# A decoder layer on one core: the first four weight steps by output block instead of by input chunk

## The chip, the cores and the metric

One core of a Trainium2 chip runs the whole program. The metric is the time of one execution on the device, in microseconds (us); before the change its median over three runs is 1454.42.

## The reference

One inference step of one layer of a hybrid decoder, for 256 prompt tokens and 8 sample tokens together (264 columns, `N`). All arithmetic is float32. What matters here is the very beginning, the combined projection of the normalized input:

```python
xn = rmsnorm(x, g_mix)          # x * rsqrt(mean(x*x) + eps) * g_mix
z = xn @ w_in                   # D = 2048 rows in 16 chunks of 128; 41 output blocks of 128 columns
xr, conv_new = causal_conv(z[..., OFF_RGX:OFF_RGG], conv_buf, conv_w, conv_b)
```

Behind it come an RG-LRU group, an mLSTM group, an output projection, cross attention over 256 memory tokens and a SwiGLU part.

## The kernel before

**Arithmetic.** Every float32 operand of a matmul is split into a high and a low half (type `fp32r`), and each product takes three matmuls: high by high, high by low, low by high (`mm3`). High halves are copies made by ScalarE (`act.activation(..., AF.Copy)`), low halves differences made by VectorE. For x the copy carries the norm weight `g_mix` of its chunk as a scale (`split`); the factor rsqrt(mean) is applied later, when a result leaves PSUM, so the sum of squares (`acc_x`) is not needed at once.

**Steps.** The program is a list of weight steps, each of up to 1 MB of weights: `load_piece` brings a step's two halves from HBM on SP's queue (tile `raw`, five buffers of 512 KB), `split_half` turns each half into high and low (tile `w`, four buffers), and TensorE multiplies. Splits run one step ahead (`LS = 1`), loads three steps ahead (`LD = 3`). Behind the start a step is one output block of 128 columns with all 16 chunks, 48 matmuls.

**The first four steps** differ, since x is not there yet. Step q holds chunks 4q to 4q+3 of x for the first four output blocks, again 48 matmuls, into four banks of PSUM (`first`). In HBM the step's weights lie as [partition, block n, chunk c, 128]. `load_first(i, c)` fetches the weights of one chunk for all four blocks, so each partition reads four runs of 512 B. `pe_first` goes by chunk outside and by block inside, so the first chunk of x and its 256 KB of weights already give 12 matmuls. `split_first` converts in the same order: a chunk of x, then that chunk's weights, eight pairs for two steps. Loads of x (`load_x`, tile `xres`) alternate with those of weights on SP's queue; chunk 0 of x and the first 16 columns of `vec` (they hold `g_mix`, tile `vecs`) come on ScalarE's queue, x first. Before all that TensorE runs eight float32 matmuls of ones on ones (`warm`), which use a tile that VectorE fills.

**Squares.** Chunks 0 to 7 of x are squared one at a time on ScalarE and added on VectorE, behind the split that is the latest one when the loop is at step 1 (`sumsq`). Chunks 8 to 15 come as two batches of four behind the split of step 4 (`last_squares`), and `norm_x` then has TensorE sum `acc_x` over the partitions inside step 5, at its chunk 9.

**Order.** SP's queue is in the order of the code. For the other engines a scheduler decides, except where `in_order()` (ScalarE and VectorE) or `manual_schedule` (TensorE, here from step 4 to step 6) keep the code's order.

Of the kernel before, what the change touches and what calls it, by code (L numbers as in the profile page):

```python
# [10 lines left out]
F32 = mybir.dt.float32  # L11
# [83 lines left out]
def layer_kernel(ctx: ExitStack, tc, xT, memT, vec, wrg, w_in, w_out, w_q, w_k, w_v, w_o,  # L95
# [12 lines left out]
    def in_order():  # L108
        return tc.manual_schedule(engines={mybir.EngineType.Activation, mybir.EngineType.DVE})
# [8 lines left out]
    def B(shape, dt=F32):  # L118
        return sb.tile(shape, dt, tag="B", bufs=NB, name=nm("B"))
# [85 lines left out]
            dve.tensor_sub(wl[:, :nch], r[:, :nch], wh[:, :nch].bitcast(F32))  # L205
        splits[i, h] = (wh, wl)

    def load_first(i, c):

        if c % 2 == 0:  # L210
            raws.setdefault(i, []).append(raw_half())
        r = raws[i][c // 2][:, c % 2 * 512: c % 2 * 512 + 512]
        sp.dma_start(r.rearrange("p (n m) -> p n m", m=P),
                     steps[i][0].rearrange("p (n c m) -> p c n m", c=4, m=P)[:, c])

    def split_first(i, h):

        wh, wl = wrows(sb.tile([P, WW], F32R, tag="w", bufs=4, name=nm("w")), i)
        r = raws[i][h].rearrange("p (c m) -> p c m", m=P)
        with tc.high_priority(), in_order():  # L220
            for c in range(2):
                x, k = 4 * i + 2 * h + c, slice(4 * c, 4 * c + 4)
                split(*xn(x), xres[:, x, :], V("g_mix", x))
                st["split"] = act.activation(wh[:, k], r[:, k], AF.Copy)
                dve.tensor_sub(wl[:, k], r[:, k], wh[:, k].bitcast(F32))
        splits[i, h] = (wh, wl)

    def last_squares():

        a, b = (B([P, BW])[:, 0: 4 * N] for _ in range(2))  # L230
        for t, q in ((a, 2), (b, 3)):
            act.activation(t, xres[:, 4 * q: 4 * q + 4, :].rearrange("p c n -> p (c n)"), AF.Square)
        dve.tensor_add(a, a, b)
        dve.tensor_add(a[:, 0: 2 * N], a[:, 0: 2 * N], a[:, 2 * N:])
        dve.tensor_add(a[:, 0: N], a[:, 0: N], a[:, N: 2 * N])
        dve.tensor_add(acc_x, acc_x, a[:, 0: N])

    def wrows(w, i):

# [32 lines left out]
    def mm3(ps, a, b, start, stop):  # L272
        ah, al = a
        bh, bl = b
        ps, bh, bl = by2(ps), turn(bh), turn(bl)
        pe.matmul(ps, ah, bh, start=start, stop=False)
        pe.matmul(ps, ah, bl, start=False, stop=False)
        pe.matmul(ps, al, bh, start=False, stop=stop)
# [58 lines left out]
    def warm(n, w=None):  # L337

        ps = bank()
        for _ in range(n):  # L340
            pe.matmul(ps[:, :P], ones if w is None else w.to_broadcast([P, P]), ones, start=True, stop=True)

    warm(8)
    onesr = const.tile([P, P], F32R, name="onesr")
    mask = const.tile([P, P], F32, name="mask")
    pick = const.tile([P, 2 * H - 1], F32, name="pick")
# [6 lines left out]
    def V(name, j=0, w=1):  # L353
        o = _V[name][0] + j
        return vecs[:, o: o + w]
# [648 lines left out]
    def pe_first(q):  # L1004
        def f(i):
            w = W(i)
            for c in range(4):
                for n in range(4):
                    mm3(first[n][:, :N], w(4 * c + n), rx(4 * q + c), q + c == 0, q + c == 6)
        return f  # L1010

    def evac_first(_):
# [425 lines left out]
    def load_x(e, lo, hi):  # L1438
        e.dma_start(xres[:, lo:hi, :], xT[:, lo:hi, :])

    for c in range(4):
        load_first(0, c)
        if c == 0:
            load_x(sp, 1, 2)
        elif c == 1:
            load_x(sp, 2, 4)
    for i in range(1, 3):
        for c in range(0, 4, 2):
            load_x(sp, 4 * i + c, 4 * i + c + 2)
            load_first(i, c)  # L1450
            load_first(i, c + 1)
        if i == 1:
            sp.dma_start(vecs[:, 16:], vec[:, 16:])
    with tc.high_priority(), in_order():
        load_x(act, 0, 1)
        act.dma_start(vecs[:, 0:16], vec[:, 0:16])
        act.activation(warm_act, ones[:, 0:1], AF.Square)
        split_half(0, 0)
        split_half(0, 1)
# [4 lines left out]
    for i, (src, cols, pef, evf, need) in enumerate(steps):  # L1464
        if i > 1:
            load_piece(i + LD - 1)
        if i == 7:
            st["rg"] = side(rg_gen(), 0)
        if "pend" in need:
            with tc.high_priority(300):  # L1470
                for e, x in pend:
                    e(x)
            pend = []
        for q in need:
            if q in st:
                finish(lambda: st[q].done)
        if not 4 <= i < 7:
            with tc.high_priority(300):
                for e, x in pend:
                    e(x)  # L1480
            pend = []
        if i == len(steps) - 1:
            kept.enter_context(tc.manual_schedule(engines={mybir.EngineType.PE}))
        now = pe.clock
        dve.clock, act.clock = max(dve.clock, now), max(act.clock, now)
        split_half(i + LS, 0)
        if i + LS < len(steps) and steps[i + LS][1] > 1024:
            split_half(i + LS, 1)
        if i == 4:
            kept.enter_context(tc.manual_schedule(engines={mybir.EngineType.PE}))  # L1490
        ps = pef(i)
        if i == 6:
            kept.close()
        if i == 1:
            with tc.issue_after(st["split"].ins):
                for c in range(8):
                    sumsq(acc_x, xres[:, c, :], c == 0)
        if i == 3:
            with tc.issue_after(st["split"].ins), tc.high_priority():
                last_squares()  # L1500
            st["rstd_x"] = Gen(norm_x())
        if evf is not None:
            pend.append((evf, ps))
        if i == 0:
            for c in range(0, 4, 2):
                load_x(sp, 12 + c, 14 + c)
                load_first(3, c)
                load_first(3, c + 1)
        else:
            load_piece(i + LD)  # L1510
        pump(pe.clock + SLACK)
        if i == 24:
            st["ng"] = side(ml_norm(), 6)
        if i == 57:
            PACE["full"] = False
        if i == 44:
            pool_e.dma_start(kept_k, ml["kb"])
            for q in range(2):
                pool_e.dma_start(kept_v[q], ml["vts"][q])
        if i == 40:  # L1520
            st["memg"] = side(mem_gen(), 7)
# [117 lines left out]
```

## Time and profile before

| what | us |
|---|---|
| median of three runs (lowest, highest) | 1454.42 (1454.29, 1455.89) |
| profiled execution: span from first to last instruction | 1452.1 |
| median less this span | 2.3 |
| TensorE busy | 1439.9 |
| VectorE, ScalarE busy | 1046.0, 793.6 |

The page gives the profiled execution's own time only as its span. In its rows PE is TensorE's matmul side, PEld its weight loads, DVE VectorE, ACT ScalarE, POOL GpSimd, SP the sync engine; a q behind a name is the queue of that engine's own issues. A row of the timeline has its start, its duration, the engine, the source line (L60 is a helper that issues all operations), the operation with out<-in by tile name, and how many like it were merged; in brackets stands how long the engine was idle before it and what ended that. Busy times of TensorE are modelled from pipelined matmuls, so a pause shows as a gap between starts rather than as a small share.

### The profile page before, as it was taken

What the parts mean: (1) busy time and instruction counts of PE and PEld (TensorE: products, weight loads), DVE (VectorE), ACT (ScalarE), POOL (GpSimd) and SP (SyncE); (2) the same over time, 40 slices, a digit from 0 to 9 for tenths busy, and PEclk for the clock granted to TensorE, in tenths of its full rate; (3) what the DMA queues carried; (4) which work ended last, traced back from release to release, by engine and by line L of the source; (5) the groups of instructions that cost most, each with busy time, mean ns of one, the idle gap of its engine ahead of it and who ended that gap; (6) DMA issues with size and microseconds to landing.
All of it is one profiled execution on the core that took longest, in us unless ns stands there. A gap on an engine that the chain in (4) does not pass through costs nothing.

```text
span 1452.1 us, 30115 instructions
## 1 busy us (share of the span) xinstructions
PE 1439.9 (99%) x12059; PEld 1415.4 (97%) x12059; DVE 1046.0 (72%) x1999; ACT 793.6 (55%) x1279; POOL 129.4 (9%) x206
## 2 busy tenths in 40 slices
PE   9999999999999999999999999999999999999997
PEld 8999999999999999999999999999999999999997
DVE  7966798898899999977676665555665655556564
ACT  7678686665556666656544444344444434444463
POOL 0001210000124343410000000000000000000000
PEclk9999999999999999999999999999999999999999
DMA  9755897558799977956555565655555655656573
GB/s 289 234 171 187 289 356 259 175 171 280 268 328 360 340 287 288 361 175 203 191 196 195 194 199 192 199 193 197 194 199 193 196 198 193 199 191 198 165 239 126
DMA packets 100765, 329.18 MB, mean 227 GB/s; under 512 B 11056, under 2 KB 19936, under 8 KB 100624
## 3 DMA queue, kind: packets, MB, share of 16 engines
q1 hardware_dynamic: 84336, 271.95, 56.3%
q0 software_dynamic: 15424, 54.22, 10.4%
q8 instruction: 94, 1.54, 0.4%
q10 hardware_dynamic: 864, 1.09, 0.2%
q14 instruction: 47, 0.39, 0.1%
HBM read 314.36 MB, written 12.86 MB: 225 GB/s over the span
## 4 chain that ended last, share of the span: by engine, by line
PE 56%; issue 2%; DVE 2%; DMA 1%; POOL 0%; ACT 0%; DVEq 0%; POOLq 0%; ACTq 0%
PE mm L60 55%; PE ax L60 1%; DVE B L60 1%; DMA B<-kcT 1%; DVE dw L60 0%; DVE w L60 0%; POOL ds L1189 0%; ACT B L60 0%; ACT dw L60 0%; ACT w L60 0%; POOL B L1243 0%; DVE t L60 0%; DVE c L60 0%; POOL o_v L1287 0%; ACT ds L60 0%
## 5 line engine op out<-in xcount | busy, mean ns | idle before, releaser
L60 PE MATMUL mm<-B,w 128*128 128x264 f32 (+1 forms) x10960 | 1282.1, 279 | 0.5 <-DVE w L60 0.5
L60 PEld LDWEIGHTS mm<-B,w 128*128 128x128 f32 x10960 | 1262.1, 189 | 8.3 <-DVE w L60 0.9
L60 DVE TENSOR_TENSOR w<-raw,w 128x1024 fp32r<-128x1024 f32 (+1 forms) x522 | 625.2, 1199 | 308.2 <-ACT w L60 307.4
L60 ACT ACTIVATE w<-raw 128x1024 fp32r<-128x1024 f32 (+1 forms) x522 | 535.1, 1028 | 518.9 <-PE mm L60 352.1
L60 PE MATMUL mm<-w,B 128*128 128x512 f32 x384 | 86.6, 380 | 0.0
L60 PEld LDWEIGHTS mm<-w,B 128*128 128x128 f32 x384 | 70.7, 189 | 9.4
L1528 POOL TENSOR_TENSOR B<-B,rstd 128x264 f32<-128x264 f32 x4 | 2.8, 736 | 802.8 <-ACT rstd L60 802.8
L60 DVE TENSOR_TENSOR t<-mm,rstd 128x264 f32<-128x264 f32 x96 | 41.4, 432 | 28.5 <-PE mm L60 28.3
L60 DVE SCALAR_TENSOR_TENSOR B<-B,dw 128x256 f32<-128x256 f32 x128 | 53.4, 470 | 3.2 <-ACT dw L60 3.0
L60 DVE TENSOR_TENSOR xres<-xres,mm 128x264 f32<-128x264 f32 (+1 forms) x81 | 34.2, 424 | 29.2 <-PE mm L60 29.2
L60 DVE SCALAR_TENSOR_TENSOR dw<-B,qsm,dw 128x256 f32<-128x256 f32 x96 | 49.1, 516 | 1.7 <-ACT dw L60 0.9
L1189 POOL TENSOR_TENSOR ds<-dw,ds 128x256 fp32r<-128x256 f32 x32 | 36.1, 1128 | 106.0 <-ACT ds L60 96.9
L60 PE MATMUL ax<-B,B 128*128 128x256 f32 (+3 forms) x280 | 44.4, 301 | 0.0
L60 PEld LDWEIGHTS ax<-B,B 128*128 128x128 f32 x280 | 39.0, 191 | 2.2
L60 ACT ACTIVATE B<-xres,vecs 128x264 fp32r<-128x264 f32 (+1 forms) x64 | 32.2, 502 | 3.2 <-DVE xres L60 1.7
L60 ACT ACTIVATE t<-xres 128x264 f32<-128x264 f32 (+1 forms) x53 | 21.0, 408 | 15.9 <-DVE xres L60 15.9
L60 ACT ACTIVATE dw<-B,qsm 128x256 f32<-128x256 f32 x32 | 16.2, 507 | 22.8 <-issue 10.0
L1178 POOL DMA_DIRECT2D B<-kcT x32 | 17.3, 541 | 116.4 <-DVE B L60 103.3
L60 ACT ACTIVATE dw<-B,B 128x128 f32<-128x128 f32 x64 | 21.0, 391 | 11.7 <-DMA B<-scr 9.1
L60 DVE SCALAR_TENSOR_TENSOR B<-xres,vecs,B 128x264 fp32r<-128x264 f32 x48 | 23.4, 489 | 4.0 <-ACT B L60 3.9
L60 ACT ACTIVATE dw<-ax,dw 128x256 f32<-128x256 f32 x32 | 15.0, 471 | 18.7 <-DVE dw L60 16.6
L60 ACT ACTIVATE B<-t 128x264 fp32r<-128x264 f32 (+1 forms) x60 | 24.1, 409 | 2.1 <-DVE t L60 2.1
(173 smaller groups left out, 693.2 us busy)
## 6 DMA issues: line engine op xcount, KB each, us to landing
raw<-w_gu SPq DMA_DIRECT2D x176, 512.0 KB, 4.2
raw<-w_d SPq DMA_DIRECT2D x80, 512.0 KB, 4.3
raw<-w_in SPq DMA_DIRECT2D x74, 512.0 KB, 5.2
raw<-w_out SPq DMA_DIRECT2D x32, 512.0 KB, 4.1
B<-kcT POOLq DMA_DIRECT2D x32, 512.0 KB, 8.8
raw<-w_q SPq DMA_DIRECT2D x32, 512.0 KB, 5.8
B<-vcT POOLq DMA_DIRECT2D x32, 512.0 KB, 9.6
raw<-w_k SPq DMA_DIRECT2D x32, 512.0 KB, 5.2
```

What stands on the lines that cost most here:

```text
L60: return f(*a, **k)
L1178: pool_e.dma_start(kc, kcT[h, b])
L1189: pool_e.tensor_sub(ws[:, 1], acc, ws[:, 0].bitcast(F32))
L1528: e.tensor_mul(st["y"](c), st["y"](c), r)
```

## The change

It does six things. (1) The four chunks of a step's weights are loaded by output block: block n of the step is one piece of 2 KB per partition, `load_first(i, n, k)` loads k blocks at once, and from the third block of step 0 on a load takes two blocks, 4 KB per partition. (2) x is loaded in fours (two chunks at the start), and three of the first four chunks' places change: chunks 0 and 1 come on ScalarE's queue behind the norm weights, chunks 2 and 3 second on SP's. (3) `pe_first` goes by block outside and by chunk inside; for the first block of step 0 it does four high by high, four high by low and four low by high. (4) `split_first` converts all four chunks of x first, then the weights, in pieces of two blocks (in step 0 of one block); the high half of the very first piece is copied by VectorE. (5) All squares come in four batches of four chunks, two behind the splits of step 4 (the fifth block) and two behind those of step 5. (6) The warm-up has seven matmuls on a constant that is there at program start. TensorE's order is now kept from step 0 on.

```diff
-    def load_first(i, c):
-
-        if c % 2 == 0:
+    def load_first(i, n, k=1):
+
+        if n % 2 == 0:
             raws.setdefault(i, []).append(raw_half())
-        r = raws[i][c // 2][:, c % 2 * 512: c % 2 * 512 + 512]
-        sp.dma_start(r.rearrange("p (n m) -> p n m", m=P),
-                     steps[i][0].rearrange("p (n c m) -> p c n m", c=4, m=P)[:, c])
+        o = n % 2 * 512
+        sp.dma_start(raws[i][n // 2][:, o: o + k * 512], steps[i][0][:, n * 512: (n + k) * 512])
...
         with tc.high_priority(), in_order():
-            for c in range(2):
-                x, k = 4 * i + 2 * h + c, slice(4 * c, 4 * c + 4)
-                split(*xn(x), xres[:, x, :], V("g_mix", x))
-                st["split"] = act.activation(wh[:, k], r[:, k], AF.Copy)
+            parts = (slice(0, 4), slice(4, 8)) if i == 0 else (slice(0, 8),)
+            if i + h == 0:
+                dve.tensor_copy(wh[:, 0:4], r[:, 0:4])
+            if h == 0:
+                for x in range(4 * i, 4 * i + 4):
+                    split(*xn(x), xres[:, x, :], V("g_mix", x))
+            for k in parts:
+                if i + h + k.start > 0:
+                    st["split"] = act.activation(wh[:, k], r[:, k], AF.Copy)
                 dve.tensor_sub(wl[:, k], r[:, k], wh[:, k].bitcast(F32))
...
+    def squares(q):
+
+        t = B([P, BW])[:, 0: 4 * N]
+        act.activation(t, xres[:, 4 * q: 4 * q + 4, :].rearrange("p c n -> p (c n)"), AF.Square)
+        dve.tensor_add(t[:, 0: 2 * N], t[:, 0: 2 * N], t[:, 2 * N:])
+        if q == 0:
+            dve.tensor_add(acc_x, t[:, 0: N], t[:, N: 2 * N])
+            return
+        dve.tensor_add(t[:, 0: N], t[:, 0: N], t[:, N: 2 * N])
+        dve.tensor_add(acc_x, acc_x, t[:, 0: N])
...
-    warm(8)
+    warm(7, nc.const_aps.tensor(1.0, [P, P], F32))
...
-            for c in range(4):
-                for n in range(4):
-                    mm3(first[n][:, :N], w(4 * c + n), rx(4 * q + c), q + c == 0, q + c == 6)
+            for n in range(4):
+                ps = first[n][:, :N]
+                if q + n == 0:
+                    for k, l in ((0, 0), (0, 1), (1, 0)):
+                        for c in range(4):
+                            pe.matmul(by2(ps), w(c)[k], turn(rx(c)[l]), start=k + l + c == 0, stop=False)
+                    continue
+                for c in range(4):
+                    mm3(ps, w(4 * n + c), rx(4 * q + c), q + c == 0, q + c == 6)
...
     with tc.high_priority(), in_order():
+        act.dma_start(vecs[:, 0:16], vec[:, 0:16])
         load_x(act, 0, 1)
-        act.dma_start(vecs[:, 0:16], vec[:, 0:16])
+        load_x(act, 1, 2)
...
-        if i == 1:
-            with tc.issue_after(st["split"].ins):
-                for c in range(8):
-                    sumsq(acc_x, xres[:, c, :], c == 0)
-        if i == 3:
+        if i in (3, 4):
             with tc.issue_after(st["split"].ins), tc.high_priority():
-                last_squares()
-            st["rstd_x"] = Gen(norm_x())
+                for q in range(2):
+                    squares(2 * i - 6 + q)
+            if i == 4:
+                st["rstd_x"] = Gen(norm_x())
```

What this does to the order can be seen at three places. The first is SP's queue at program start, before (`raw` are weights, `xres` is x, `vecs` the other vectors; a piece in the form 4x128 is read in runs of 512 B):

```order
L213 DMA raw_117<-w_in 128x4x128
L1439 DMA xres<-xT 128x264
L213 DMA raw_117<-w_in 128x4x128
L1439 DMA xres<-xT 128x528
L213 DMA raw_122<-w_in 128x4x128 x2
L1439 DMA xres<-xT 128x528
L213 DMA raw_126<-w_in 128x4x128 x2
L1439 DMA xres<-xT 128x528
L213 DMA raw_130<-w_in 128x4x128 x2
```

And the same queue after:

```order
L213 DMA raw_116<-w_in 128x512
L1450 DMA xres<-xT 128x528
L213 DMA raw_116<-w_in 128x512
L213 DMA raw_120<-w_in 128x1024
L1450 DMA xres<-xT 128x1056
L213 DMA raw_123<-w_in 128x1024
L213 DMA raw_125<-w_in 128x1024
```

Seven loads now bring what thirteen brought, and x of step 1 stands ahead of all its weights. The second place is ScalarE from its first split on, before (`B` are halves of x where `xres` is read, `w` the high weights):

```order
L60 ACTIVATE B_150<-xres,vecs 128x264
L60 ACTIVATE w_147<-raw_117 128x4x128
L60 ACTIVATE B_150<-xres,vecs 128x264
L60 ACTIVATE w_147<-raw_117 128x4x128
L60 ACTIVATE B_150<-xres,vecs 128x264
L60 ACTIVATE w_161<-raw_122 128x4x128
L60 ACTIVATE B_150<-xres,vecs 128x264
L60 ACTIVATE w_161<-raw_122 128x4x128
```

After, from the same place, with step 1 behind it:

```order
L60 ACTIVATE B_143<-xres,vecs 128x264 x4
L60 ACTIVATE w_139<-raw_116 128x4x128
L60 ACTIVATE w_157<-raw_120 128x4x128 x2
L60 ACTIVATE B_169<-xres,vecs 128x264 x4
L60 ACTIVATE w_166<-raw_123 128x8x128
L60 ACTIVATE w_182<-raw_125 128x8x128
```

The four chunks of x stand together ahead of the weights, and one copy has gone to VectorE. The third place is ScalarE around the squares: before, the first of them stood between the weights of step 2 and the x of step 3 (`acc_x` and `t` are single squares):

```order
L60 ACTIVATE w_270<-raw_139 128x4x128
L60 ACTIVATE acc_x<-xres 128x264
L60 ACTIVATE t_331<-xres 128x264
L60 ACTIVATE t_334<-xres 128x264
L60 ACTIVATE t_337<-xres 128x264
L60 ACTIVATE t_340<-xres 128x264
L60 ACTIVATE t_343<-xres 128x264
L60 ACTIVATE t_346<-xres 128x264
L60 ACTIVATE B_359<-xres,vecs 128x264
```

After, the squares stand behind the weights of steps 4 (`w_391`, `w_394`) and 5 (`w_458`, `w_461`):

```order
L60 ACTIVATE w_391<-raw_313 128x8x128
L60 ACTIVATE w_394<-raw_315 128x8x128
L60 ACTIVATE B_445<-xres 128x1056
L60 ACTIVATE B_449<-xres 128x1056
L60 ACTIVATE w_458<-raw_387 128x8x128
L60 ACTIVATE w_461<-raw_389 128x8x128
L60 ACTIVATE B_513<-xres 128x1056
L60 ACTIVATE B_518<-xres 128x1056
```

No square is left ahead of the x of step 3. Behind these places, from the gates of the ninth block on, every engine's list of operations is the same in both kernels.

More of the change, by code (lines that the diff above doesn't have):

```diff
@@ L220, in split_first @@
         with tc.high_priority(), in_order():
-            for c in range(2):
-                x, k = 4 * i + 2 * h + c, slice(4 * c, 4 * c + 4)
-                split(*xn(x), xres[:, x, :], V("g_mix", x))
-                st["split"] = act.activation(wh[:, k], r[:, k], AF.Copy)
+            parts = (slice(0, 4), slice(4, 8)) if i == 0 else (slice(0, 8),)
[7 more added lines that the diff above has]
+                    st["split"] = act.activation(wh[:, k], r[:, k], AF.Copy)
                 dve.tensor_sub(wl[:, k], r[:, k], wh[:, k].bitcast(F32))
         splits[i, h] = (wh, wl)
[L228 to L236, printed above, removed]
+    def squares(q):
[7 more added lines that the diff above has]
+        dve.tensor_add(acc_x, acc_x, t[:, 0: N])
     def wrows(w, i):
@@ L340, in warm @@
         for _ in range(n):
-            pe.matmul(ps[:, :P], ones if w is None else w.to_broadcast([P, P]), ones, start=True, stop=True)
-    warm(8)
+            pe.matmul(ps[:, :P], w, w, start=True, stop=True)
+    warm(7, nc.const_aps.tensor(1.0, [P, P], F32))
     onesr = const.tile([P, P], F32R, name="onesr")
@@ L1439, in load_x @@
         e.dma_start(xres[:, lo:hi, :], xT[:, lo:hi, :])
[L1441 to L1446, printed above, removed]
+    load_first(0, 0)
+    load_x(sp, 2, 4)
+    load_first(0, 1)
+    load_first(0, 2, 2)
     for i in range(1, 3):
[L1448 to L1451, printed above, removed]
+        load_x(sp, 4 * i, 4 * i + 4)
+        load_first(i, 0, 2)
+        load_first(i, 2, 2)
         if i == 1:
@@ L1488, in layer_kernel @@
             split_half(i + LS, 1)
-        if i == 4:
+        if i == 0:
             kept.enter_context(tc.manual_schedule(engines={mybir.EngineType.PE}))
@@ L1504, in layer_kernel @@
         if i == 0:
[L1505 to L1508, printed above, removed]
+            load_x(sp, 12, 16)
+            load_first(3, 0, 2)
+            load_first(3, 2, 2)
         else:
```

## Prediction

> **What bounds the kernel now.** I read the page first, then the chain of waits, then the list of waits cut to the first 60 us, and last the timeline of those microseconds. The page, and of the chain two pieces ahead of 650 and its two longest:
>
> ```profile
> span 1452.1 us, 30115 instructions
> PE 1439.9 (99%) x12059; PEld 1415.4 (97%) x12059; DVE 1046.0 (72%) x1999; ACT 793.6 (55%) x1279; POOL 129.4 (9%) x206
> ...
> 567.91 1.46 POOL ds L1189
> ...
> 615.05 1.30 DVE B L60 x7
> ...
> 650.03 80.33 PE mm L60 x714
> 730.81 707.06 PE mm L60 x6285
> ```
>
> TensorE is busy for 99% of the span, and its order of work is nearly fixed. One matmul with 264 columns costs 80.33 / 714 = 0.1125 us; 707.06 / 6285 gives the same. The change adds no such matmul and takes none away. So the time can move only by what TensorE waits, and the order of every engine behind the squares of x is the same in both kernels. What the start gains or loses is then carried as a shift to the end. The timeline of the start, in a few places (start, duration, engine, idle time before it and its releaser):
>
> ```profile
> 0.90 0.17 DVE L60 MEMSET ones<- 128x128 f32 x1 [0.90 <-PEq L1611]
> ...
> 1.12 3.78 PE L60 MATMUL mm<-ones 128*128 128x128 f32 x16 [1.12 <-DVE ones L60]
> ...
> 1.22 0.45 ACTq L1456 DMA_DIRECT2D vecs<-vec  x1
> ...
> 1.53 0.60 SPq L1439 DMA_DIRECT2D xres<-xT  x1
> ...
> 1.70 1.28 ACT L60 ACT_TABLE_LOAD   x1 [1.70 <-PEq L1611]
> ...
> 4.02 0.52 ACT L60 ACTIVATE B<-xres,vecs 128x264 fp32r<-128x264 f32 x1 [0.82 <-DMA vecs<-vec]
> 4.44 0.61 ACT L60 ACTIVATE w<-raw 128x512 fp32r<-128x512 f32 x1
> ...
> 5.11 1.19 PE L60 MATMUL ax<-B,w 128*128 128x264 f32 x6 [0.21 <-ACT w L60]
> ...
> 6.93 0.52 ACT L60 ACTIVATE B<-xres,vecs 128x264 fp32r<-128x264 f32 x1
> ...
> 11.44 0.94 PE L60 MATMUL ax<-B,w 128*128 128x264 f32 x6
> ...
> 20.98 1.97 ACT L60 ACTIVATE t<-xres 128x264 f32<-128x264 f32 x6
> ...
> 22.86 0.50 ACT L60 ACTIVATE B<-xres,vecs 128x264 fp32r<-128x264 f32 x1
> 23.27 0.61 ACT L60 ACTIVATE w<-raw 128x512 fp32r<-128x512 f32 x1
> ...
> 23.93 0.60 PE L60 MATMUL ax<-B,w 128*128 128x264 f32 x3 [1.10 <-ACT w L60]
> ```
>
> Real work starts at 5.11, and the first matmul of step 3 at 23.93. In between lie steps 0 to 2, 144 matmuls, 16.20 us of work. TensorE has thus lost 23.93 - 16.20 = 7.73 us: 5.11 ahead of the first and 2.62 in gaps, the last of them 1.10 us behind six squares of x on ScalarE. From 23.93 to 40 it pauses no more. The waits and the traffic of the first 40 us (in 1 us slices) say who is late:
>
> ```profile
> ACT w L60 <- DMA raw<-w_in: 4.4, 8, 1.8
> DVE w L60 <- ACT w L60: 3.7, 9, 0.7
> PEld ax L60 <- ACT w L60: 2.3, 4, 1.3
> ...
> GB/s 0 20 242 299 174 335 297 301 348 321 343 319 309 351 312 309 334 314 330 325 311 335 313 360 394 410 377 262 340 94 295 238 197 295 283 324 283 209 266 221
> ```
>
> TensorE waits for ScalarE's copies and these for the loads. From slice 6 on the traffic stands near 325 GB/s, and it steps up to 394, 410 and 377 in slices 24 to 26, when the pieces in 512 B runs end and those in 4 KB runs begin.
>
> **The change part by part.** What counts is when step 3 starts; I follow the one chain that sets it. Prices (count, busy and mean ns), and the time from issue to landing of the first loads of x:
>
> ```profile
> L60 ACT ACTIVATE w<-raw 128x1024 fp32r<-128x1024 f32 x13 | 13.3, 1049 | 4.8 <-PE mm L60 2.9 <-DMA raw<-w_in 1.8
> L60 DVE TENSOR_TENSOR w<-raw,w 128x1024 fp32r<-128x1024 f32 x11 | 13.3, 1221 | 0.6 <-ACT w L60 0.6
> L60 DVE TENSOR_TENSOR w<-raw,w 128x512 fp32r<-128x512 f32 x18 | 12.4, 689 | 3.4 <-ACT w L60 3.1
> L60 DVE SCALAR_TENSOR_TENSOR B<-xres,vecs,B 128x264 fp32r<-128x264 f32 x16 | 7.8, 489 | 4.0 <-ACT B L60 3.9
> ...
> xres<-xT SPq DMA_DIRECT2D x1, 264.0 KB, 4.1
> xres<-xT ACTq DMA_DIRECT2D x1, 132.0 KB, 2.2
> xres<-xT SPq DMA_DIRECT2D x1, 132.0 KB, 2.9
> vecs<-vec ACTq DMA_DIRECT2D x1, 8.0 KB, 2.7
> ```
>
> *First matmul.* The norm weights go first, so by their 2.7 us they land at 3.5 instead of 1.22 + 2.7 = 3.9. ScalarE has one more load to issue ahead of its table load, 0.4, which then ends near 3.4 and hides under that landing. The first chunk of x is split from 3.6 to 4.1, and no ScalarE copy of weights follows that TensorE must wait for. VectorE's copy of 512 elements is not in this trace: at most the 0.69 of a two-input operation of that size, at least nothing, since it runs while ScalarE works. I take 0.5, and a start at 4.3, 0.8 earlier. The warm-up of seven needs 7/8 of 3.78 = 3.3 us, no longer waits for the tile of ones, so it starts near 0.9, and is over at 4.2.
>
> *First output block.* It needs all four chunks of x, four splits at VectorE and then its low weights. The third and fourth chunk land at 5.3 by the sum of the next part (0.81 MB; the row's 4.1 us from SP's second issue at 1.5 would give 5.6). Splits start 0.42 apart on ScalarE, so the fourth is done at 6.3; VectorE's 0.49 and 0.69 follow, to 7.5, and the four matmuls with the low weights end at 8.0. Blocks two to four follow at 12 x 0.1125 = 1.35 each: 12.05. Step 1 can start 0.6 later than its 11.44 of before: what the earlier start gains is lost again here.
>
> *Step 1 sets the path.* It needs four chunks of x and half its weights. With the x, 4 raw pieces of 256 KB, 8 chunks of 132 KB and 8 KB have come (of 1024 bytes): 2.14 MB; with the first half of the weights 2.66 MB. By 4.0 us the slices have moved 0.56 MB, and at 390 GB/s the rest takes 4.05 and 5.4 us: 8.05 and 9.4. Landing is later than that: the 132 KB on SP landed at 1.53 + 2.9 = 4.43, some 0.5 after its 0.54 MB, and the 264 KB behind it by 6.93, 0.9 after its 1.07 MB (6.0). I take 0.65: 8.7 and 10.05. x is split from 8.75 on and ScalarE is free at 10.43; the copy of 1.05 ends at 11.48, VectorE's low half of 1.22 at 12.73 (its own four splits end before), and TensorE goes on at 12.79. It has reached this point at 12.05 + 0.22, so it stalls 0.5. From there 46 matmuls of step 1 and 48 of step 2 end at 12.79 + 10.57 = 23.36.
>
> On the rate this rests on, the row comes first: 325 GB/s in short runs, 394 in long ones. [...]
>
> *Steps 2 and 3.* By the same sum step 2's x (3.95 MB, other vectors among it) lands at 13.35 and its weights (4.48 MB) at 14.7; they are split by 17.5 and wanted at 17.96. Step 3's land by 18.9, are split by 21.5 and wanted at 23.36. The squares no longer stand there, so the 1.10 gap goes. What is late next is only the stall of step 1.
>
> *Queues.* SP issues 14 loads instead of 25 up to those of step 3; they are larger, so the queue reaches the later weights sooner. Later loads wait for the raw tiles to come free, as now. Cost nothing, hidden under the traffic.
>
> *Squares.* Eight single ones and their adds leave the ramp; four batches come instead, two behind the splits of the fifth block and two behind those of the sixth.
>
> ```profile
> 28.87 2.04 ACT L60 ACTIVATE B<-xres 128x1056 f32<-128x1056 f32 x2
> ...
> 35.48 0.43 DVE L60 TENSOR_TENSOR acc_x<-acc_x,B 128x264 f32<-128x264 f32 x1
> ...
> 38.05 0.72 PE L60 MATMUL ax<-ones,acc_x 128*128 128x1 f32 x6
> ```
>
> Now the sum is ready at 35.9 and TensorE asks at 38.05: 2.1 us to spare. After: the sixth block's second half needs the buffer that step 3 frees at 28.8; copy to 29.8, squares (1.02 each, start to start) to 31.9, adds and interleaved low halves to about 34.5; asked for at 38.05 - 0.57 = 37.5. The cover is 3 us, so I cost it at nothing.
>
> **Sum.** 23.93 - 23.36 = 0.57 gained. The profiled execution has 1452.1 of span, and the median of 1454.42 lies 2.3 above it; I keep that: 1454.42 - 0.57 = 1453.8 us. What a measurement here can tell from no change is about 0.2%, 2.9 us.
>
> **The rivals.** (a) *Longer runs bring no faster traffic*, and TensorE now waits for twice as much data at the head of each step. By the row of slices 2.66 MB are there at 10.95 and land at 11.6; copy and low half take it to 13.95. Step 2's weights (4.48 MB, 16.6) come out at 19.6, and 46 matmuls on step 3 starts at 24.8: 0.9 slower, 1455.3. It decides once the rate stays under about 350. For it: half of step 0's pieces have 2 KB runs, which no row prices. Against: slices 24 to 26.
>
> (b) *TensorE's clock halves in the thin first block.* The trace has one such place (a timeline row, then half-microsecond stretches of TensorE; last columns: granted clock, DMA share, GB/s):
>
> ```profile
> 161.78 0.83 PE L60 MATMUL ax<-ones,B 128*128 128x1 f32 x6 [1.56 <-DVE B L60]
> ...
> 162.50:163.00 0.50, 0.50 (x5) 0.66 0.93 107
> 163.00:163.50 0.50, 0.50 (x4) 0.50 0.66 131
> ...
> 166.00:166.50 0.50, 0.50 (x6) 0.93 0.75 180
> ```
>
> A pause of 1.56 us and then tiny matmuls brought 0.50 from about 162.66 to 166.07, as the shares 0.66 and 0.93 tell, so for 3.4 us; the pause of 1.10 at 22.8 left the rate of matmuls as it was. The first block does 1.35 us of work in the 3.7 from 4.3 to 8.0, in pauses of half a microsecond. Half clock for 3.4 us takes 1.7 us, of which the stall of 0.5 is there anyway: 1.2 - 0.57 = 0.6 slower, 1455.0. [...]
>
> (c) *Loads come earlier than I reckon*, step 1 does not stall and step 0 ends at 11.4 as now: step 3 at 11.4 + 10.8 = 22.2, 1.7 gained, 1452.7.
>
> (d) *The stages up to 650 swallow the shift*: ahead of that the chain runs over POOL and DVE as well, as the two pieces show. Their work is released by TensorE's, so I doubt it: 1454.4.
>
> (e) *The sum of squares comes late*: it decides once the sixth block's weights are over 3 us late, and a pause of 2 us with (b)'s half clock costs 3.7: 1454.42 - 0.57 + 3.7 = 1457.6.
>
> **How the numbers follow.** Forecast 0.45, (a) 0.17, (b) 0.12, (c) 0.15, (d) 0.07, (e) 0.04. From (c) less half a microsecond, to (a) with a little spread of the runs (1454.29 to 1455.89), the range is 1452.2 to 1455.9. Faster than 1451.5 only something beyond (c): 0.06; slower than 1457.3 is (e), or (a) with (b): 0.05; within 0.2%: 0.89.
>
> **What would show it.** Right: first real matmul near 4.3, traffic near 390 GB/s from slice 6 on, a short wait of TensorE for `w` near 12.5, step 3 from 23.4, none behind it to 38. Wrong: slices at 325 (a); a granted clock of 0.50 before 15 us (b); step 3 before 22.5 (c); TensorE waiting ahead of the sums of `acc_x` (e).

## The result and the profile after

The changed kernel is slower: 1458.17 us median against 1454.66 us for the kernel before, ratio 1.0025 with a 95% interval of 1.0015 to 1.0036. Measured a second time, it came out at 1456.80 against 1455.03, ratio 1.0012 [1.0003, 1.0021]. The loss is 1.8 to 3.5 us, more than rival (a)'s 0.9 and about as much as rival (e)'s 3.2, but from another cause than either. The profiled execution took 1462.21 us, with a span of 1460.5; it was the longest of its six.

First the page and the piece of the chain that starts the long last run of matmuls (start, duration), to be held against 1452.1 and 650.03 of before:

```profile
span 1460.5 us, 30069 instructions
PE 1443.9 (99%) x12057; PEld 1418.8 (97%) x12057; DVE 1044.9 (72%) x1994; ACT 792.1 (54%) x1266; POOL 129.6 (9%) x206
...
658.26 80.33 PE mm L60 x714
```

From that piece to the end it takes 802.2 us, before 802.1. So in these two traces 8.2 us are lost ahead of it. The timeline of the start says how the first of them went:

```profile
0.84 3.33 PE L60 MATMUL mm<-const-float32-1.0 128*128 128x128 f32 x14 [0.84 <-PEq L1617]
...
4.30 0.43 DVE L60 CAST w<-raw 128x512 fp32r<-128x512 f32 x1 [3.23 <-DMA raw<-w_in]
...
5.56 0.52 ACT L60 ACTIVATE B<-xres,vecs 128x264 fp32r<-128x264 f32 x1 [1.85 <-DMA xres<-xT]
...
6.12 0.59 PE L60 MATMUL ax<-B,w 128*128 128x264 f32 x1 [1.95 <-ACT B L60]
...
6.58 1.33 ACT L60 ACTIVATE B<-xres,vecs 128x264 fp32r<-128x264 f32 x3 [0.51 <-DMA xres<-xT]
...
7.15 7.43 PE L60 MATMUL ax<-B,w 128*128 128x264 f32 x35 [0.44 <-ACT B L60]
...
8.35 2.49 DVE L60 TENSOR_TENSOR w<-raw,w 128x512 fp32r<-128x512 f32 x4
...
12.38 1.22 DVE L60 TENSOR_TENSOR w<-raw,w 128x1024 fp32r<-128x1024 f32 x1
...
15.77 4.21 PE L60 MATMUL ax<-B,w 128*128 128x264 f32 x36
...
26.57 4.21 PE L60 MATMUL ax<-B,w 128*128 128x264 f32 x36
...
40.41 0.72 PE L60 MATMUL ax<-ones,acc_x 128*128 128x1 f32 x6
```

The warm-up ends at 4.17, and TensorE then waits 1.95 us for the first chunk of x. Behind 7.15 three matmuls follow each other by 0.38 to 0.41 us, the pace of ScalarE's copies of x. From 8.34 on TensorE waits for nothing that the profile shows, and yet its matmuls start 0.22 us apart up to 13.22: the 35 from 7.15 on take 7.43 us where 36 take 4.21 later. VectorE has the low halves of all of step 0's weights at 8.35 + 2.49 = 10.84; the first half of step 1's is there at 13.60, and TensorE comes to step 1 only at 15.77. Step 3 starts at 26.57 (before: 23.93), the sums of `acc_x` come at 40.41 (before: 38.05): 2.36 us late. The first loads (KB each, us from issue to landing) and the traffic in 1 us slices:

```profile
xres<-xT SPq DMA_DIRECT2D x1, 264.0 KB, 4.0
raw<-w_in SPq DMA_DIRECT2D x1, 256.0 KB, 3.5
xres<-xT ACTq DMA_DIRECT2D x1, 132.0 KB, 4.2
vecs<-vec ACTq DMA_DIRECT2D x1, 8.0 KB, 3.7
...
GB/s 0 31 137 309 344 336 425 417 406 418 407 425 394 410 401 410 422 422 414 410 406 406 385 397 188 258 213 147 315 98 340 164 53 303 193 82 324 135 16 193
```

From slice 6 to slice 23 the traffic is 385 to 425 GB/s, as forecast. But what was issued first landed later than in the kernel before: the norm weights took 3.7 us instead of 2.7, the first chunk of x 4.2 instead of 2.2.

The other 5.9 us (8.2 less 2.36) lie nearly all between 165 and 195. The three pauses of TensorE there, and its pace behind the last (columns: TensorE's issue and busy time with the count of matmuls, granted clock, DMA share, GB/s):

```profile
164.19 0.83 PE L60 MATMUL ax<-ones,B 128*128 128x1 f32 x6 [1.56 <-DVE B L60]
171.23 1.57 PE L60 MATMUL ax<-B,B 128*128 128x256 f32 x8 [1.82 <-ACT B L60]
186.63 2.18 PE L60 MATMUL ax<-B,B 128*128 128x256 f32 x8 [1.91 <-ACT B L60]
...
185.00:190.00 5.00, 3.37 (x15) 0.74 1.01 405
190.00:195.00 5.00, 5.00 (x27) 0.57 1.03 397
```

Before had the first of these only, and half clock for 3.4 us behind it; here it is half from 187 to about 194. Whether the change makes the other two is a question for the experiments.

### The profile page after: what moved, and what is told of

Same layout as the page of the kernel before. It is cut to its first block, busy times and chain, and to the rows that moved or that the text cites. A ratio compares the mean times of both kernels' runs of the same rounds, so it can differ in the third digit from the quotient of the medians.

```text
span 1460.5 us, 30069 instructions
## 1 busy us (share of the span) xinstructions
PE 1443.9 (99%) x12057; PEld 1418.8 (97%) x12057; DVE 1044.9 (72%) x1994; ACT 792.1 (54%) x1266; POOL 129.6 (9%) x206
## 4 chain that ended last, share of the span: by engine, by line
PE 56%; DVE 1%; issue 1%; POOL 0%; DMA 0%; ACT 0%; DVEq 0%; POOLq 0%; ACTq 0%
PE mm L60 55%; PE ax L60 1%; DVE B L60 1%; DVE dw L60 0%; DMA o_k<-t 0%; DVE w L60 0%; POOL ds L1200 0%; POOL B L1254 0%; ACT B L60 0%; DVE c L60 0%; POOL o_v L1298 0%; DVE t L60 0%; ACT ds L60 0%; DVEq L1622 0%; ACT c L60 0%
```

## The experiments

Three theories for the start, and one for the rest. **C, the clock:** TensorE works at half its pace (0.22 us from start to start instead of 0.11) through the thin first block and beyond. **Q, the queue:** long rows on SP's queue hold back ScalarE's queue, so x comes late (x0 is its first chunk). **V:** it is the norm weights, in short rows, that hold back what stands behind them on ScalarE's queue. **D:** the stage from 150 to 195 us decides, and by itself. Each kernel is listed with its first real matmul, the number of gaps of 0.20 to 0.27 us between the starts of successive matmuls from 5 to 17 us (of real work; the normal gap is 0.11, and a single one of 0.22 also followed waits at full clock, as the three of the first trace of before did), the start of the sums of `acc_x`, and its median and ratio to the kernel before, timed alongside (whose own median was between 1454.65 and 1455.22 each time):

| kernel | first | slow gaps | sums | us | ratio [95%] |
|---|---|---|---|---|---|
| before (first trace, again) | 5.11, 5.22 | 3, 6 | 38.05, 39.35 | 1454.66 | 1 |
| after | 6.12 | 22 | 40.41 | 1458.17 | 1.0025 [1.0015, 1.0036] |
| after, again | 6.08 | 13 | 39.73 | 1456.80 | 1.0012 [1.0003, 1.0021] |
| after, warm-up 12 | 6.02 | 10 | 39.66 | 1456.18 | 1.0006 [0.9994, 1.0019] |
| after, warm-up 20 | 7.96 | 1 | 38.46 | 1454.92 | 0.9999 [0.9990, 1.0008] |
| after, x on SP | 4.98 | 21 | 39.32 | 1457.07 | 1.0017 [1.0008, 1.0026] |
| after, x on SP, warm-up 16 | 6.59 | 5 | 39.37 | 1456.55 | 1.0009 [1.0000, 1.0018] |
| after, 512 B runs | 5.38 | 20 | 39.96 | 1456.29 | 1.0007 [0.9998, 1.0016] |
| before, vecs first | 5.45 | 2 | 38.84 | 1454.58 | 0.9999 [0.9990, 1.0008] |
| before, 2 KB runs | 6.08 | 1 | 36.23 | 1454.07 | 0.9999 [0.9990, 1.0007] |
| the same, x0 on SP | 4.95 | 5 | 36.43 | 1453.61 | 0.9992 [0.9983, 1.0000] |
| the same, squares late | 4.75 | 8 | 37.74 | 1454.76 | 0.9999 [0.9991, 1.0008] |
| before, squares late | 5.19 | 5 | 40.28 | 1457.42 | 1.0017 [1.0008, 1.0025] |

### The clock: a longer warm-up

```diff
-    warm(7, nc.const_aps.tensor(1.0, [P, P], F32))
+    warm(12, nc.const_aps.tensor(1.0, [P, P], F32))
```

> The changed kernel with twelve warm-up matmuls instead of seven; nothing else. Theory C (clock): the pause of 1.95 us ahead of the first real matmul keeps TensorE at half clock until about 13.3, and that is most of the 2.4 us lost by the sums of squares. Then TensorE is busy until about 6.2, reaches full clock by 8 at the latest, step 1 starts near 13.6 instead of 15.77, the sums near 38.2 instead of 40.4, and the ratio to the kernel before falls from 1.0025 to about 1.001. Rival L (landing): the late x alone sets the pace and the clock costs nothing; step 1 starts within 0.3 us of 15.77 and the ratio stays at 1.0025.

The sums came at 39.66 instead of the 38.2 expected, only 0.75 earlier than in the changed kernel. Twelve matmuls end at 5.43; two pauses follow, of 0.58 and 1.36 us, with a single matmul between them, and from 8.95 to 11.19 the gaps are 0.22 again. TensorE's pace (stretch; TensorE's issue and busy time with the count of matmuls, granted clock, DMA share, GB/s):

```profile
4.00:5.00 1.00, 1.00 (x9) 1.00 1.03 336
...
6.00:8.00 2.00, 0.62 (x2) 0.94 1.04 400
8.00:10.00 2.00, 2.00 (x8) 0.50 1.02 375
10.00:12.00 2.00, 2.00 (x15) 0.70 1.02 396
```

The nine matmuls from 4 to 5 us are at full pace already: this warm-up reached it, and behind the two pauses it was gone again. The shares 0.94 and 0.70 put the half clock from about 7.8 to 11.2, so 3.4 us. What this run does not tell is what a warm-up without a pause behind it would give. One of 20 lasts until x is there:

```diff
-    warm(7, nc.const_aps.tensor(1.0, [P, P], F32))
+    warm(20, nc.const_aps.tensor(1.0, [P, P], F32))
```

> The changed kernel with twenty warm-up matmuls instead of seven. In the changed kernel's trace 23 matmuls stand 0.22 us apart from 8.3 to 13.3 us, and 0.11 apart from then on, though every input was ready by 10.9. Theory C, the clock: with TensorE busy up to 7.1 us these matmuls run 0.11 apart, the first output block ends when its last low weights are ready, near 9.5, and step 1 starts near 13.3 instead of 15.77; sums of acc_x near 38.0 instead of 40.4, and 1454.2 to 1455.8 us. Theory Q alone, late first loads without a lasting loss of clock: step 1 stays where the warm-up of twelve left it, 15.0, or moves later with the longer warm-up; 1456 to 1457. Theory D, the stage from 150 to 200 us decides the time: the time does not follow the start.

Its timeline, and TensorE's pace in stretches of 2 us:

```profile
5.74 0.52 ACT L60 ACTIVATE B<-xres,vecs 128x264 fp32r<-128x264 f32 x1 [2.03 <-DMA xres<-xT]
...
6.71 1.33 ACT L60 ACTIVATE B<-xres,vecs 128x264 fp32r<-128x264 f32 x3 [0.45 <-DMA xres<-xT]
...
7.96 4.67 PE L60 MATMUL ax<-B,w 128*128 128x264 f32 x36
...
13.82 0.39 PE L60 MATMUL ax<-B,w 128*128 128x264 f32 x2
```

```profile
8.00:10.00 2.00, 1.89 (x17) 1.00 1.03 385
10.00:12.00 2.00, 2.00 (x20) 1.00 1.00 386
12.00:14.00 2.00, 2.00 (x20) 1.00 1.03 413
```

The same stretches of the changed kernel:

```profile
8.00:10.00 2.00, 2.00 (x10) 1.00 1.01 412
10.00:12.00 2.00, 2.00 (x11) 1.00 1.04 416
12.00:14.00 2.00, 2.00 (x14) 1.00 1.03 402
```

x came no earlier (its copies start at 5.74 and 6.71, against 5.56 and 6.58), and real work began 1.84 us later, at 7.96. Yet step 1 started at 13.82 instead of 15.77, the sums at 38.46 instead of 40.41, and the time is that of the kernel before. This is theory C: 36 matmuls took 4.67 us once TensorE had not paused ahead of them. Against the second trace of the changed kernel, below, the sums gain 1.27 instead of 1.95.

That it is the granted clock shows in the second trace of the changed kernel:

> The changed kernel once more, unaltered, for a second trace of it. What comes from the change must come again: x0 and x1 landing 4 us and more after their issue, over 15 matmuls 0.22 us apart in the first output block, sums of acc_x at 39.5 to 41, without a wait of TensorE for acc_x. What the first trace lost beyond its start (two pauses of 1.8 and 1.9 us behind the scratch round trips between 165 and 190 us, and half clock behind the second) need not: by the theory that this part varies from execution to execution, the stretch from the sums to the last piece of the ramp of mixing steps, 617.9 us in the first trace, lies between 612 and 615 this time. If the change causes it, 616 or more again.

```profile
8.00:10.00 2.00, 1.98 (x9) 0.57 1.04 389
10.00:12.00 2.00, 2.00 (x12) 0.58 1.01 402
12.00:14.00 2.00, 2.00 (x20) 1.00 1.01 406
```

Here the column falls to 0.57 and 0.58 over 8 to 12 us (13 slow gaps, 8.64 to 11.52, where over 15 were expected). The two shares put the half clock from about 8.3 to 11.7, 3.4 us again. In the first trace the column stands at 1.00 throughout the start, though the pace is the same. Nor does it show the slow pace of the warm-up: in the first traces of before and after it stands at 1.00 over the first 5 us, where 16 matmuls took 3.78 us and 14 took 3.33. Why was not shown; at these starts the pace is read from the starts of the matmuls.

Of theory D, the same trace has this:

```profile
163.31 0.83 PE L60 MATMUL ax<-ones,B 128*128 128x1 f32 x6 [1.56 <-DVE B L60]
183.71 1.57 PE L60 MATMUL ax<-B,B 128*128 128x256 f32 x8 [0.30 <-ACT B L60]
```

The pauses of 1.82 and 1.91 have not come again. From the sums to the 714 matmuls it took 651.80 - 39.73 = 612.1, against 617.9 in the first trace; so the 5.9 us do not come with the change each time. The kernel before, traced again, agrees:

> The kernel before once more, unaltered, for a second trace of it: x0 lands 2.2 us after its issue and the norm weights 2.7 (within 0.4), first matmul 5.0 to 5.4, sums of acc_x 37.8 to 38.5. By the theory that the stage from 150 to 190 us varies by itself, its pauses differ from those of the first trace, where there was one of 1.56 us. If the first trace is typical, the stretch from the sums to the last piece of the mixing steps is 612.0 again, within 0.5.

It paused 1.34 and 0.67 us in this stage and needed 649.77 - 39.35 = 610.4 (first trace: 612.0; 612.0 within 0.5 was expected). Its start varies too: step 2 waited 1.00 us for a copy whose load was late, the pause ahead of step 3, behind the squares, came again with 1.07, and its sums came at 39.35, later than the 37.8 to 38.5 expected. The first trace, with a single gap of 1.10, was an early one. So the starts of single traces of one kernel differ by 0.7 (after) to 1.3 us (before), and smaller differences between variants prove nothing.

Nor do the pauses need the change: the kernel before with the norm weights first, the next run, has all three, of 1.55, 1.96 and 1.39 us, and took 614.6 us for the stretch. The second of them:

```profile
169.63 1.58 PE L60 MATMUL ax<-B,B 128*128 128x256 f32 x8 [1.96 <-ACT B L60]
```

### The queue: who holds back x

> The kernel before with one part of the change alone: the norm weights ahead of the first chunk of x on ScalarE's queue. Theory V (the norm weights' rows of 64 B hold up what stands behind them): x lands more than 1 us later than its 3.0, the norm weights at 0.8 + 3.7, first real matmul near 6 instead of 5.11, and the time is 1 us or more longer. Theory Q: SP's rows are 512 B here, so x loses only its 0.4 us of issue, the norm weights land by 3.5, first real matmul at 5.1 or a little earlier, time unchanged within 0.5 us.

```profile
xres<-xT ACTq DMA_DIRECT2D x1, 132.0 KB, 3.1
```

The norm weights ahead of x0, in the kernel before, landed 1.7 us after their issue, x0 3.1; first matmul 5.45 instead of 5.11, the time unchanged. x0 landed at 4.28 instead of 3.03, so 1.25 later: 0.4 of issue, as Q had it, and 0.9 of a longer wait, as V had it. V's other signs (late norm weights, first matmul near 6, a longer time) did not come. The second place in the queue is thus worth 0.9 of the 2.0 us that are to be explained, and V alone does not explain them. Next, the kernel before with nothing changed but the runs in HBM:

```diff
-        sp.dma_start(r.rearrange("p (n m) -> p n m", m=P),
-                     steps[i][0].rearrange("p (n c m) -> p c n m", c=4, m=P)[:, c])
+        sp.dma_start(r, steps[i][0][:, c * 512: c * 512 + 512])
...
+    w_in[0:4] = w_in[0:4].reshape(4, P, 4, 4, P).transpose(0, 1, 3, 2, 4).reshape(4, P, 2048).copy()
```

> The kernel before, with the weights of the first four steps laid out in HBM by chunk, so that each load by chunk reads one run of 2 KB per partition instead of four of 512 B; order, queues and sizes as before. Theory R (longer runs are what the change gains, and the order by block is what it loses): traffic near 400 GB/s instead of 325 from slice 6 on, the waits for loads go, first real matmul between 5.1 and 5.6 (Q: x on ScalarE's queue lands later than 3.0), step 3 starts near 22.5 instead of 23.93, ratio 0.999. Rival (the rate does not matter because ScalarE and VectorE pace the start): step 3 within 0.3 of 23.93, ratio 1.000.

```profile
xres<-xT ACTq DMA_DIRECT2D x1, 132.0 KB, 3.4
...
vecs<-vec ACTq DMA_DIRECT2D x1, 8.0 KB, 3.7
```

x0 now took 3.4 us instead of 2.2 and the norm weights 3.7 instead of 2.7, though both queues issue the same loads in the same order. That is theory Q. SP also issued its loads closer together, the third at 1.72 instead of 2.17; whether the rows or the earlier loads hold back ScalarE's queue is not separated. Theory R held for the start, though not for the first matmul (6.08): step 3 started at 22.39, and TensorE waited for nothing behind 6.08. The time was that of the rival, 0.9999. The changed kernel has long runs and a first matmul at 6.12 too, and its sums come 3.5 to 4.2 us later: what it loses, it loses by the rest of the change. No run here has the order by block alone, so the order, the places of x and the shorter warm-up are not told apart, except as far as the warm-up of 20 does it. The reverse, the changed kernel back in runs of 512 B:

```diff
-        o = n % 2 * 512
-        sp.dma_start(raws[i][n // 2][:, o: o + k * 512], steps[i][0][:, n * 512: (n + k) * 512])
+        for m in range(n, n + k):
+            o = m % 2 * 512
+            sp.dma_start(raws[i][n // 2][:, o: o + 512].rearrange("p (c m) -> p c m", m=P),
+                         steps[i][0].rearrange("p (c n m) -> p n c m", n=4, m=P)[:, m])
...
+    w_in[0:4] = w_in[0:4].reshape(4, P, 4, 4, P).transpose(0, 1, 3, 2, 4).reshape(4, P, 2048).copy()
```

> The changed kernel with its pieces of weights in 512 B runs again (one load for each output block, so six more issues on SP's queue; order of matmuls, of the first loads and of the squares as changed). Theory Q, long runs on SP's queue hold back ScalarE's: norm weights and x0 land 0.7 to 1.2 us sooner, by 3.8 and 4.4 instead of 4.5 and 5.5, the first matmul at 5.0; the traffic then stays near 325 GB/s and the weights of the later steps come later, sums of acc_x at 40 to 42 and a wait for acc_x possible: 1457 to 1460 us. If run length does not matter to ScalarE's queue: x0 at 5.5 again, first matmul at 6.1.

```profile
xres<-xT ACTq DMA_DIRECT2D x1, 132.0 KB, 3.4
vecs<-vec ACTq DMA_DIRECT2D x1, 8.0 KB, 1.7
```

There were seven more issues on SP's queue, not six. The queue did as Q says (1.7 instead of 3.7, 3.4 instead of 4.2, first matmul 5.38). The rest of the expectation was wrong: the time came out at 1456.29, no worse than with long runs. TensorE waited for no load after 7.01, and 20 matmuls ran at half pace as before; that it could not have used faster traffic fits this, but is argued. In the first 12 us the profile's packets on SP's queue average 0.65 KB in the kernel before and 1.76 KB in 2 KB runs (2.86 MB in 4415, 3.27 MB in 1861); by what mechanism ScalarE's queue is held back was not shown.

x0 and x1 ahead of everything on SP's queue, in the changed kernel:

```diff
+    load_x(sp, 0, 2)
     load_first(0, 0)
...
-        load_x(act, 0, 1)
-        load_x(act, 1, 2)
```

> The changed kernel with chunks 0 and 1 of x as the first load on SP's queue, ahead of the weights, and only the norm weights on ScalarE's. [...] Rival B (it is the bytes in flight, whatever the queue): the first weights and the norm weights come later in exchange, first real matmul not before 5.7, ratio 1.002.

x landed 2.9 us after its issue and the first matmul came at 4.98, 1.14 earlier than in the changed kernel and ahead of rival B's 5.7. But step 1 gained no more than that (14.68 instead of 15.77, sums 39.32 instead of 40.41): 20 gaps stayed slow, from 7.46 to 11.89, and chunks 2 and 3, now third on SP's queue, landed at 6.08 instead of 5.29, so that the wait only moved behind the second matmul:

```profile
6.11 0.92 ACT L60 ACTIVATE B<-xres,vecs 128x264 fp32r<-128x264 f32 x2 [1.25 <-DMA xres<-xT]
```

An earlier x alone is worth 0.4 to 1.1 us of the start, by the two traces of the changed kernel, and the time does not tell it from nothing (1.0017, between 1.0025 and 1.0012). With a longer warm-up as well:

> The changed kernel with the first two chunks of x ahead of everything on SP's queue and sixteen warm-up matmuls. With seven of them that order of loads put the first real matmul at 4.98, but 20 matmuls ran 0.22 apart up to 11.9, and step 1 began at 14.68. Theory C: the warm-up ends at 6.2, no matmul from 7 on stands 0.22 apart, step 1 starts at 12.5 and the sums at 37.1, 1 us ahead of the kernel before: 1453.3 to 1454.5 us. If only the loads matter: step 1 at 14.7 or later, 1456 to 1457.5. Theory D: the sums come at 37.1 and the time is still that of the kernel before or more, 1454.5 to 1456.

No run of slow gaps was left, only five single ones beside waits, and step 0 was through by 13.05; but now step 1 waited twice, up to 14.85 (0.77 us for VectorE's low half of `w`). Sums at 39.37: a miss for C's numbers (37.1), not for its pace. That the x ahead of them on SP's queue made its weights late is argued.

The same move in the kernel before with 2 KB runs, x0 alone:

```diff
+    load_x(sp, 0, 1)
     for c in range(4):
         load_first(0, c)
...
-        load_x(act, 0, 1)
         act.dma_start(vecs[:, 0:16], vec[:, 0:16])
```

> The kernel before with its pieces of weights in 2 KB runs (its order of matmuls kept) and the first chunk of x ahead of them on SP's queue, the norm weights alone on ScalarE's. With 2 KB runs alone the first chunk of x landed 3.4 us after its issue and the first matmul came at 6.08, the sums at 36.2. Theory Q: the chunk of x lands by 3.7 and the norm weights by 4.2, first matmul at 5.1 to 5.3, and since the order by chunk needs one chunk at a time the rate stays full: sums at 35.4 if the later loads keep up, 36.2 if they do not. If the place of x in the queues does not matter: first matmul near 6.1. Theory D puts the time at 1453.3 to 1454.4 whichever it is; if the start counts in full, 1451.8 to 1452.6.

First matmul at 4.95, but five gaps were slow and there was one wait of 0.41 for the second piece of weights, so that the sums stayed at 36.43. At 1453.61 it is the fastest of all, 0.08% ahead of the kernel before timed alongside (1455.22), an interval that reaches 1.0000. Its sums are 1.6 to 2.9 us earlier than in the two traces of before, and the time 1.6 shorter.

### The squares

The kernel before with the squares alone moved, as in the change:

> The kernel before with one part of the change alone: the squares of x in four batches behind blocks five and six; loads, their runs and the order of matmuls as before. My costing: the pause of 1.10 us ahead of step 3 goes, the sums of acc_x come at 36.95 instead of 38.05 without a wait of TensorE for them, and the time falls by up to 1.1, to 1453.5. Rival: the loads in 512 B runs are late there anyway, the pause only moves from ScalarE's squares to its copies: sums at 37.7 to 38.1, 1454.3 to 1454.8. Rival with the other sign: the batches delay the sums and TensorE waits for acc_x by 1 to 3 us: 1455.5 to 1457.5.

The timeline at the sums, and TensorE's pace behind them:

```profile
39.80 0.43 DVE L60 TENSOR_TENSOR acc_x<-acc_x,B 128x264 f32<-128x264 f32 x1
...
40.28 1.44 PE L60 MATMUL ax<-ones,acc_x 128*128 128x1 f32 x6 [2.40 <-DVE acc_x L60]
```

```profile
38.00:40.00 2.00, 0.00 (x0) 1.00 0.44 168
40.00:42.00 2.00, 1.72 (x8) 0.55 0.94 297
42.00:44.00 2.00, 2.00 (x11) 0.50 0.90 307
44.00:46.00 2.00, 2.00 (x11) 0.50 0.30 115
46.00:48.00 2.00, 2.00 (x15) 0.75 0.00 0
```

My costing missed, and the rival with the other sign came. This is rival (e) as it was drawn, a wait of 2.40 us and then half clock to about 47, only in a kernel that has the old loads. The median is 2.2 us up. In long runs it is milder:

> The kernel before with pieces of weights in 2 KB runs and the first chunk of x on SP's queue, as run earlier, and now the squares of x in batches behind blocks five and six as well. In 512 B runs this move made TensorE wait 2.4 us for acc_x and then work at half clock for 6.8 us. Theory cover: it was the late weights of the sixth block that made them late; in long runs the weights wait for TensorE and not the other way, acc_x is ready 1 us or more ahead of the sums, which stay at 36.4, and the time is that of the kernel without the move, 1453 to 1454. Rival: the batches take too much of VectorE's time whichever way the loads come; then acc_x is ready near 38, TensorE waits 1 to 2 us and its clock halves: 1455 to 1457.

```profile
37.74 0.83 PE L60 MATMUL ax<-ones,acc_x 128*128 128x1 f32 x6 [1.11 <-DVE acc_x L60]
```

A wait of 1.11 us and 1454.76 (0.9999) where the same kernel without the move had 1453.61 (0.9992); the intervals overlap, so the time alone does not tell the two apart. The rival holds by its wait, though no half clock followed, and the cover theory falls for this order of loads. In the changed kernel and all its variants traced here TensorE does not wait for `acc_x`. In the first trace the last add ends at 38.09 + 0.43 = 38.52, 1.9 us ahead of the sums at 40.41.

## Why the prediction was wrong

**What held.** TensorE bounds the kernel, and what the start loses is carried to the end: in twelve of the fourteen traces the stretch from the sums to the 714 matmuls took 610.4 to 614.6 us, whenever the sums came (the others: 617.9 in the first trace of the changed kernel, 617.0 with half clock behind the sums in the kernel before with the squares late). It is no shorter where the sums come late, so rival (d) fell, though 2 KB runs alone brought the sums 1.8 to 3.1 us forward and the time only 0.6. The traffic near 390 GB/s from slice 6 held; rival (a) fell. The squares cost nothing in the changed kernel; the cover was 1.9 us, not 3.

**The first step that failed** is *First matmul*: "a start at 4.3". It took the landing of the norm weights (2.7 us) from a queue that ran beside 512 B rows, and gave none to x0 of its own behind them. Beside 2 KB rows they took 3.7, and x0, which now stood second, 4.2 from its issue at 1.25. The copy of x0 started at 5.56, not 3.6, and the first matmul at 6.12. The two swaps of run length and that of the places separate the parts: x0 took 2.2 us in first place beside short rows, 3.1 and 3.4 in second place beside short rows, 3.4 in first place beside long ones and 4.2 in second place beside long ones. So the place costs 0.8 to 1.2 us and the run length as much again. The corner values repeat: 2.2 in three traces with the loads of before, 4.1 to 4.4 in four with those of after; the two between have one trace for each swap.

**The step that cost most** is *First output block*: "Blocks two to four follow at 12 x 0.1125 = 1.35 each: 12.05". The step also had its inputs too early: it reckoned with chunks 2 and 3 of x, which landed at 5.29 as forecast, and not with chunk 1, second of the two on ScalarE's queue, which landed at 6.56; so ScalarE's fourth split ended at 7.91 instead of 6.3. And the price of a matmul is right only at full clock. The first block's inputs were all split by 9.0 (8.35 and a quarter of 2.49; forecast 7.5), but its matmuls and those of the next blocks ran 0.22 apart up to 13.22, so 22 gaps of 0.11 too much, 2.4 us. This is rival (b), which had the half clock and a chance of 0.12. It was sized at 3.4 us of half clock, the length read off the trace of before, 1.7 us lost, and half a microsecond of that was thought hidden in the stall of step 1. There was no stall to hide it. In the second trace and with the warm-up of twelve the half clock lasted 3.4 us, as (b) had it; in the first trace the slow stretch lasted from 8.34 to 13.22. Its warm-up never came to full pace (14 matmuls of the profile in 3.33 us, where the later ones of longer warm-ups start 0.11 apart), and thin work up to 8.34 did not bring it either; that this made the stretch longer is argued. The number of slow matmuls varied: 22 and 13 slow gaps in two executions of one kernel. Taking the half pace away by the warm-up of 20 gave 1.95 us back against the first trace and 1.27 against the second. The sums were forecast for 37.48 and came at 40.41: 2.93 late, 1.95 of it the clock by this swap; the remaining 0.98 is the late x, or what the longer warm-up itself cost.

**Step 1 sets the path** failed with it: no wait for `w` came near 12.5, because TensorE reached step 1 2.2 us after the first half of its weights was split. That half was ready at 13.60 instead of 12.73, since VectorE was at step 0's low halves until 10.84 and its four splits of x came behind them.

**The size of the whole.** Forecast -0.57; the start gives +2.36 by the first pair of traces, and +0.4 to +2.4 by the two of each kernel. The measured +1.8 lies within that, and +3.5 is 1.1 above it. This remainder has no cause shown here; the stage at 150 to 195 can hold it, and it was not isolated.

## What to carry to other kernels

The start that needs more inputs before its first dense run of matmuls came with a loss of TensorE's pace as well as a wait here (22 and 13 slow gaps of 0.11 us too much, one with the warm-up of 20), so price the first block at half pace unless the warm-up lasts until the last of its inputs is there. The landing time of one load was no constant here: x0 took 2.2 us, 3.4 when the rows on another queue became longer and 3.1 in second place, so a load on which the start hangs belongs at the head of the queue with the long rows (x0 and x1 landed 2.9 us after their issue there, x0 4.2 behind the norm weights on ScalarE's). Work that is moved out of a gap, like these squares, must be priced where it arrives, in the loads of that kernel: here TensorE did not wait for them in the variants of the changed kernel, and waited 2.40 and 1.11 us in those of the kernel before.

## What the runs showed of the hardware

- With longer rows on SP's queue (2 KB instead of 512 B) the traffic rose from about 325 GB/s to between 330 and 418 in the kernel before (slices 6 to 23; 385 to 425 with rows of 2 to 4 KB in the changed kernel), and the first loads on ScalarE's queue took longer: 132 KB from 2.2 to 3.4 us, 8 KB of norm weights from 2.7 to 3.7. First in their queue, the norm weights took 3.7 beside long rows and 1.7 beside short ones.
- The longer warm-ups came to full pace at different times. All three began at 0.84 or 0.85; that of twelve ran at half pace until about 4.4, that of sixteen (with x on SP's queue) until about 5.4, that of twenty until about 6.4.
- A pause of 1.56 us ahead of tiny matmuls was followed by half clock in the second trace of the changed kernel (0.50 from about 165.3) and by none in the first (1.00 over 164 to 169). A pause of 1.39 us ahead of dense work, in the kernel before with 2 KB runs, cost one slow gap only; there TensorE went on at full pace from 6.08, where the changed kernel, from 6.12 on, had 22 slow gaps.
